# Index and attention scores of two heads as 64-row products on the two halves of the TensorE array

## The chip, the cores and the metric

The kernel runs on one core of a Trainium2 chip: TensorE (PE, with its weight loads shown apart as PEld), VectorE (DVE), ScalarE (ACT), GpSimd (POOL) and SyncE (SP), which issues the DMAs. The metric is the device time of one execution in microseconds. Three runs of the kernel before gave 1805.31, 1814.39 and 1805.31 us, so the median is 1805.31 us.

## The reference, cut to what matters

One layer of a hybrid decoder is computed for 1024 prompt tokens and 8 sampled tokens. Two of its parts are touched by the change, and both are products of queries and keys over a head dimension of 64:

```python
def select_keys(iq, ik, iw, qpos, topk):              # 8 index heads of 64, one key head
    dots = jnp.einsum('bqhd,bsd->bqhs', iq, ik)
    score = jnp.einsum('bqhs,bqh->bqs', jax.nn.relu(dots * IDX_DIM ** -0.5), iw) * IDX_HEADS ** -0.5
    ...                                                # causal mask, then the 256 best keys of each query
def sparse_attend(q, ksel, vsel, valid):              # 8 heads of 64 in two groups, one key head each
    logits = jnp.einsum('bqngd,bqknd->bqngk', qg, ksel) * HEAD_DIM_A ** -0.5
    ...                                                # mask, softmax, product with the values
```

The projections, the gated delta branch, the merge, the feed-forward part and the caches' work are as they were.

## The kernel before, in words

All in float32. A float32 operand is held in two parts, hi (rounded to the one-pass type fp32r) and lo (what is left), and a product is the sum of products of parts. `split` makes the two parts: ACT writes hi, DVE subtracts for lo.

Scores are made in two stages. **The index stage** (about 52 to 185 us of the span): for each of the query tiles i = 2 to 7 (128 queries), `scores` makes, per index head, the products with the 128·(i+1) keys so far, in one chunk up to 512 keys and in two halves above. ACT takes the relu, DVE sums over the heads with the weights. Beside it run the projections of later tiles and of z as filler (`mm3`, lines 163 to 165, tile `pj`), which keep TensorE fed. **The attention stage** (about 650 to 880 us): for each query tile i = 7 down to 0 and each of two groups of four heads, `att_scores` makes the logits of a head the same way (chunks into tile `PT`), DVE adds the mask and takes the row minimum, ACT takes the exponential, and then one of the two scales by the sum. `ORDER` is the order of these steps for four heads (0 = score, 1 = exp, 2 = norm). `att_out` transposes the weights (L1055, `PT` too) and multiplies by the values (L1059, L1060); it is woven with the scores of the next group, and the gates' projections and the sampled tokens' state update are filler.

How a score is made: `stack_q` puts hi of a head's 64 query rows on partitions 0 to 63 and lo on 64 to 127 for even heads, the other way round for odd heads. The keys stand doubled, the same 64 rows on both halves, hi in one plane and lo in another (`ik2`, `k2`). So two products of 128 rows, one with each plane, sum all four products of parts (L410 and L411 in the index stage, L1023 and L1024 in attention).

```python
nc.tensor.matmul(p, lhs, self.ik2[:, 0, c0:c1], start=True, stop=False)
nc.tensor.matmul(p, lhs, self.ik2[:, 1, c0:c1], start=False, stop=True)
```

The code's order is not the order on the engines: a scheduler (`schedule_with_timeline_sim`) puts the instructions of each engine into a fixed order when the program is built, from its own idea of when operands and buffers come free. PSUM holds 3 buffers of tile `ac` for the index scores and 5 of `PT` for attention.

Of the kernel before, what the change touches and what calls it, by code (L numbers as in the profile page):

```python
# [9 lines left out]
F32 = mybir.dt.float32  # L10
F32R = mybir.dt.float32r
# [3 lines left out]
AF = mybir.ActivationFunctionType  # L15
ALU = mybir.AluOpType
# [4 lines left out]
T = 1032  # L21
# [22 lines left out]

NORM_ACT = (0, 3)
RECIP = {0: 2, 2: 2}
ORDER = [(0, 0), (0, 1), (1, 0), (1, 1), (0, 3), (2, 0), (0, 2), (2, 1), (1, 2), (1, 3), (2, 2), (2, 3)]


BESIDE, PVS = 21, 8  # L50
# [4 lines left out]
class K:  # L55
# [205 lines left out]
    def stack_q(self, dst, nat, n, p):  # L261


        nc = self.nc
        m = nat.shape[1] // 2
        for j in range(m):
            nc.tensor.transpose(p[:, j, :n], nat[:, 2 * j:2 * j + 2, :].rearrange("p a b -> p (a b)"), self.ident[:n, :n])
        for e, (a, b) in enumerate(((0, 64), (64, 0))):
            nc.scalar.activation(dst[a:a + 64, e::2, :], p[a:a + 64, :m, :n], AF.Copy)
            nc.vector.tensor_tensor(dst[b:b + 64, e::2, :], p[a:a + 64, :m, :n], dst[a:a + 64, e::2, :].bitcast(F32),  # L270
                                    op=ALU.subtract)


    def p0_p1(self):
# [99 lines left out]
    def idx_proj(self, i, wA, wB):  # L374
        nc, wk, O = self.nc, self.wk, self.O
        r0, n = rows_of(i)
        nat = wk.tile([128, 592], F32, name="nat", tag="nat", bufs=2)
        for (wh, wl), c0 in ((wA, 0), (wB, 296)):
            if i < 2 and c0 == 0:
                continue  # L380
            p = self.pproj()
            self.mm3(p[:n, :296], [(self.xhi[:, k, r0:r0 + n], self.xlo[:, k, r0:r0 + n], wh[:, k], wl[:, k])
                                   for k in range(8)])
            nc.scalar.activation(nat[:n, c0:c0 + 296], p[:n, :296], AF.Copy)
        nc.vector.tensor_copy(self.ab[:n, i, :], nat[:n, 576:592])
        h0 = 8 if i < 2 else 0
        X = nat[:n, h0 * 64:576].rearrange("p (h d) -> p h d", d=64)
        self.rope(X, n, i, 1, 9 - h0)
        if i == 8:
            nc.sync.dma_start(O['ik_s'][0, :, 0, :], nat[:n, 512:576])  # L390
            nc.vector.tensor_copy(self.iqs, nat[:8, 0:576])
            return
        nc.sync.dma_start(O['ik_p'][0, 0, r0:r0 + n, :], nat[:n, 512:576])
        p = self.ptq()
        self.dup_T(nat[:n, None, 512:576], n, 1, p)
        self.split(self.ik2[:, 0, r0:r0 + n], self.ik2[:, 1, r0:r0 + n], p[:, 0, :])
        if i >= 2:
            self.iq2 = wk.tile([128, 8, 128], F32R, name="iq2", tag="iq2", bufs=2)
            self.stack_q(self.iq2, nat[:n, 0:512].rearrange("p (h d) -> p h d", d=64), n, self.ptq())

    def scores(self, i):
        nc, wk = self.nc, self.wk
        nk = 128 * (i + 1)
        ch = [(0, nk)] if nk <= 512 else [(0, nk // 2), (nk // 2, nk)]
        for c0, c1 in ch:
            Sv = self.S[:, self.soff[i] + c0:self.soff[i] + c1]
            for h in range(8):
                p = self.pacc()[:, :c1 - c0]
                lhs = self.iq2[:, h, :]
                nc.tensor.matmul(p, lhs, self.ik2[:, 0, c0:c1], start=True, stop=False)  # L410
                nc.tensor.matmul(p, lhs, self.ik2[:, 1, c0:c1], start=False, stop=True)  # L411
                r = self.relu[:, 512 * self.relu_n:512 * self.relu_n + c1 - c0]
                self.relu_n = 1 - self.relu_n
                nc.scalar.activation(r, p, AF.Relu, scale=0.125 * 8 ** -0.5)
                w = self.ab[:, i, h:h + 1]
                if h == 0:
                    nc.vector.tensor_scalar(Sv, r, w, 0.0, op0=ALU.mult, op1=ALU.add)
                else:
                    nc.vector.scalar_tensor_tensor(Sv, r, w, Sv, op0=ALU.mult, op1=ALU.add)
        d = self.S[:, self.soff[i] + 128 * i:self.soff[i] + nk]  # L420
        nc.gpsimd.affine_select(d, d, pattern=[[-1, 128]], compare_op=ALU.is_ge, fill=NEG, base=0,
                                channel_multiplier=1)
# [481 lines left out]
    def attention(self, end_x):  # L904
        nc, I = self.nc, self.I
        ps, end_ps = self.pool("fillers", space=PSUM)
        self.pq = self.pf = ps
        self.pj_bufs = 1
        self.ps, end_pa = self.pool("att", space=PSUM)
        self.ap, end_a = self.pool("att")  # L910
        self.sd, end_sd = self.pool("sampled")
        last, last_n = iter(()), 0
        for i in ATT:
            for g in range(2):
                P = [None] * 4
                weave(self.att_scores(i, g, P), 13, last, last_n)
                last, last_n = self.att_out(i, g, P), i + 2
        weave(last, last_n)
        gates = list(self.gates)
        weave(self.gate_steps(gates), 5 * len(gates), self.sample_delta(), 13)  # L920
        end_x()
        end_sd()
        mg, end_mg = self.pool("mergeg")
        self.wk, self.end_sa = self.pool("sample", side="right")
        mp, end_m = self.pool("mergeb", side="right")
        steps = self.merge_b(self.load_split(mp, self.d_ob), mg)
        self.sample = self.sample_attend(mg)
        weave(islice(self.sample, 33), 25, islice(steps, BESIDE), BESIDE)
        end_pa()
        end_ps()  # L930
        self.pj_bufs, self.tp_bufs = 5, 2
        self.open_psum("ps5")
        self.pf, self.end_pf = self.pool("psm", space=PSUM)
        self.stage = self.sp.tile([128, 2048], F32, name="rs", tag="kvb", bufs=1)
        x0 = self.sp.tile([128, 4224], F32, name="x20", tag="S", bufs=1)
        self.x2h = [x0[:, 0:4 * T].rearrange("p (j t) -> p j t", j=4)]
        self.x_T(0)
        self.pq = self.ps
        for _ in steps:
            pass  # L940
        end_m()
        end_mg()
        end_a()
# [61 lines left out]
    def att_scores(self, i, g, P):  # L1005

        nc, ap = self.nc, self.ap
        t0, nk = 128 * i, 128 * (i + 1)
        if g == 0:
            self.qn = ap.tile([128, 512], F32, name="qn", tag="qn", bufs=1)  # L1010
            nc.sync.dma_start(self.qn, self.d_q[t0:t0 + 128])
        q2 = ap.tile([128, 4, 128], F32R, name="q2", tag="q2", bufs=2)
        self.stack_q(q2, self.qn[:, 256 * g:256 * g + 256].rearrange("p (h d) -> p h d", d=64), 128, self.pT())
        ch = [(0, nk)] if nk <= 512 else [(0, nk // 2), (nk // 2, nk)]
        m0 = self.moff[i]
        st = ap.tile([128, 2, 2, 4], F32, name="st", tag="st", bufs=3)
        ng, sm = st[:, 0], st[:, 1, 0]

        def score(j):
            P[j] = ap.tile([128, T], F32, name="P", tag="P", bufs=8)  # L1020
            for c, (a, b) in enumerate(ch):
                p = self.pL()[:, :b - a]
                nc.tensor.matmul(p, q2[:, j, :], self.k2[:, g, 0, a:b], start=True, stop=False)  # L1023
                nc.tensor.matmul(p, q2[:, j, :], self.k2[:, g, 1, a:b], start=False, stop=True)  # L1024
                nc.vector.tensor_tensor_reduce(P[j][:, a:b], p, self.msk[:, m0 + a:m0 + b], -0.125,
                                               3e38 if c == 0 else ng[:, 0, j:j + 1], ALU.add, ALU.min,
                                               ng[:, c, j:j + 1])

        def exp(j):
            nc.scalar.activation(P[j][:, :nk], P[j][:, :nk], AF.Exp, scale=-1.0, bias=ng[:, len(ch) - 1, j:j + 1],  # L1030
                                 accum_out=sm[:, j:j + 1])

        def norm(j):
            if j in RECIP:
                v = sm[:, j:j + RECIP[j]]
                nc.vector.reciprocal(v, v)
            if j in NORM_ACT:
                nc.scalar.activation(P[j][:, :nk], P[j][:, :nk], AF.Copy, scale=sm[:, j:j + 1])
            else:
                nc.vector.tensor_scalar(P[j][:, :nk], P[j][:, :nk], sm[:, j:j + 1], None, op0=ALU.mult)  # L1040
        for f, j in ORDER:
            (score, exp, norm)[f](j)
            yield
# [788 lines left out]
```

## Time and profile before

| what | value |
|---|---|
| median of three runs | 1805.31 us |
| the profiled execution: its own time | 1802.74 us |
| its span, first to last instruction | 1801.0 us |
| PE busy (share of the span) | 1740.0 us (97%) |
| DVE, ACT busy | 1210.6 us, 852.1 us |
| mean granted TensorE clock | 0.995 |
| score products: index, attention | 160, 192 |

The span is shorter than the execution's time by 1.7 us, which lie around it. PE's "busy" is the union of its matmuls' modelled durations; consecutive matmuls overlap in it (a row's duration is about twice the distance to the next row's start), so the distance between starts, and not the duration, is what one matmul costs in a stream. In a row of a timeline the first number is the start in us, the second the duration, then come engine, line, operation, the tile written and those read, and the shape: `32*128` is the number of array rows and columns in use, `128x344` the operand that streams. A float32 product that isn't fp32r shows as two matmuls.

### The profile page before, as it was taken

The numbers are of one execution on the slowest core, as the hardware profiler recorded it, in microseconds if no ns is written. First come the engines' busy times: TensorE is split into PE (matmuls) and PEld (weight loads), VectorE is DVE, ScalarE is ACT, GpSimd is POOL, SyncE is SP. The second block draws the span as 40 slices with busy tenths as digits, with TensorE's granted clock in tenths as the row PEclk, the third lists the DMA queues.
The fourth block names the chain that finished last, engine by engine and source line by source line (L and its number), as shares of the span: only waits on it lengthen the run. The fifth ranks groups of instructions, "written<-read, shape, count | busy, mean of one in ns | idle before, by whom it ended". The sixth has DMA issues, their size and how long they took to land.

```text
span 1801.0 us, 31724 instructions
## 1 busy us (share of the span) xinstructions
PE 1740.0 (97%) x12276; PEld 1662.6 (92%) x12276; DVE 1210.6 (67%) x2776; ACT 852.1 (47%) x1575; POOL 42.2 (2%) x68
## 2 busy tenths in 40 slices
PE   5998999999999999999999999999999999999998
PEld 5998989999999988878899998999999999999998
DVE  7775558999899777797656477766666665733222
ACT  4567467877845345687444243433333333412012
POOL 3001100000000000000000000000000000000000
PEclk9999999999999999999999999999999999999999
DMA  6115434434546543254567434322222323732122
GB/s 194 43 35 153 130 101 145 130 113 120 159 131 167 149 137 109 84 183 141 195 235 226 138 110 135 101 81 85 82 72 75 91 72 125 223 100 73 51 80 69
DMA packets 293595, 218.01 MB, mean 121 GB/s; under 512 B 39292, under 2 KB 267456, under 8 KB 292412
## 3 DMA queue, kind: packets, MB, share of 16 engines
q1 hardware_dynamic: 291716, 205.50, 37.8%
q0 software_dynamic: 1728, 10.49, 1.7%
q8 instruction: 96, 1.57, 0.4%
q14 instruction: 55, 0.45, 0.1%
HBM read 154.17 MB, written 61.87 MB: 120 GB/s over the span
## 4 chain that ended last, share of the span: by engine, by line
PE 83%; DMA 7%; DVE 5%; ACT 3%; issue 2%; SPq 0%; ACTq 0%; DVEq 0%
PE pj L163 15%; PE pj L165 15%; PE pj L164 15%; PE A L1706 2%; PE A L1707 2%; PE A L1708 2%; PE D L1706 2%; PE F L1706 2%; PE F L1707 2%; PE D L1707 2%; PE F L1708 2%; PE D L1708 2%; PE PT L1055 1%; DMA araw<-d_act 1%; PE B L1706 1%
## 5 line engine op out<-in xcount | busy, mean ns | idle before, releaser
L163 PE MATMUL pj<-xhi,whi 128*128 128x344 f32 x912 | 297.5, 326 | 5.3 <-ACT gs L862 4.3
L165 PE MATMUL pj<-xhi,wlo 128*128 128x344 f32 x912 | 294.3, 323 | 0.0
L164 PE MATMUL pj<-xlo,whi 128*128 128x344 f32 x912 | 293.3, 322 | 0.0
L187 ACT ACTIVATE whi<-wraw 128x1024 fp32r<-128x1024 f32 (+4 forms) x126 | 115.2, 914 | 249.4 <-PE pj L164 208.0
L163 PEld LDWEIGHTS pj<-xhi,whi 128*128 128x128 f32 x912 | 171.9, 189 | 9.3 <-ACT gs L862 5.7
L164 PEld LDWEIGHTS pj<-xlo,whi 128*128 128x128 f32 x912 | 171.9, 188 | 2.0 <-issue 1.1
L165 PEld LDWEIGHTS pj<-xhi,wlo 128*128 128x128 f32 x912 | 171.9, 188 | 1.4
L164 PE MATMUL pj<-act,whi 128*128 128x344 f32 x528 | 170.3, 323 | 0.7 <-DVE act L188 0.7
L165 PE MATMUL pj<-act,wlo 128*128 128x344 f32 x528 | 168.9, 320 | 0.8 <-DVE wlo L188 0.8
L163 PE MATMUL pj<-act,whi 128*128 128x344 f32 x528 | 169.3, 322 | 0.2 <-DVE x L1768 0.2
L188 DVE TENSOR_TENSOR wlo<-wraw,whi 128x1024 fp32r<-128x1024 f32 (+3 forms) x104 | 116.2, 1118 | 54.4 <-ACT whi L187 52.7
L1768 DVE TENSOR_TENSOR x<-pj,x 128x344 f32<-128x344 f32 x96 | 48.5, 514 | 140.0 <-PE pj L165 139.9
L768 DVE TENSOR_SCALAR_CACHE_REDUCE kvb<-S,cand 128x384 bf16<-128x384 f32 (+3 forms) x128 | 103.7, 810 | 2.0
L165 PEld LDWEIGHTS pj<-act,wlo 128*128 128x128 f32 x528 | 99.2, 188 | 1.5 <-DVE wlo L188 1.3
L164 PEld LDWEIGHTS pj<-act,whi 128*128 128x128 f32 x528 | 99.2, 188 | 1.0 <-DVE act L188 1.0
L163 PEld LDWEIGHTS pj<-act,whi 128*128 128x128 f32 x528 | 99.2, 188 | 0.9 <-issue 0.4
L1706 PE MATMUL D<-hb,wx 128*128 128x258 f32 x328 | 93.0, 284 | 2.0 <-DVE E L1729 2.0
L1708 PE MATMUL D<-hb,wx 128*128 128x258 f32 x328 | 92.7, 282 | 0.7 <-DVE wx L188 0.7
L1706 PE MATMUL A<-hb,wlo 128*128 128x258 f32 x328 | 93.0, 283 | 0.0
L1707 PE MATMUL A<-hb,wlo 128*128 128x258 f32 x328 | 92.8, 283 | 0.0
L1708 PE MATMUL A<-hb,wlo 128*128 128x258 f32 x328 | 92.8, 283 | 0.0
L1707 PE MATMUL D<-hb,wx 128*128 128x258 f32 x328 | 92.6, 282 | 0.0
(587 smaller groups left out, 4790.3 us busy)
## 6 DMA issues: line engine op xcount, KB each, us to landing
wraw<-in_w_gate_up SPq DMA_DIRECT2D x50, 512.0 KB
wraw<-in_w_in SPq DMA_DIRECT2D x38, 512.0 KB
d_act<-x SPq DMA_DIRECT2D x41, 258.0 KB
araw<-d_act SPq DMA_DIRECT2D x20, 516.0 KB
d_g<-gs SPq DMA_DIRECT2D x48, 172.0 KB
wraw<-in_w_out SPq DMA_DIRECT2D x16, 512.0 KB
wraw<-in_w_branch SPq DMA_DIRECT2D x12, 512.0 KB
wraw<-in_w_down SPq DMA_DIRECT2D x16, 384.0 KB
```

The costliest lines, as they stand in the source:

```text
L163: nc.tensor.matmul(ps, lh, rh, start=(j == 0), stop=False)
L164: nc.tensor.matmul(ps, lh, rl, start=False, stop=False)
L165: nc.tensor.matmul(ps, ll, rh, start=False, stop=(j == last))
L187: self.nc.scalar.activation(hi, src, AF.Copy)
L188: self.nc.vector.tensor_tensor(lo, src, hi.bitcast(F32), op=ALU.subtract)
L768: nc.vector.tensor_scalar(junk[:r, :n], s, thr[:r, j:j + 1], 0.0, op0=ALU.is_lt, op1=ALU.add, accum_out=cnt[:r, j:j + 1])
L1055: nc.tensor.transpose(p[:, j, :], P[j][:, 128 * s:128 * s + 128], self.ident)
L1706: nc.tensor.matmul(p, lh, rh, start=(first and k == 0), stop=False, skip_group_check=True)
L1707: nc.tensor.matmul(p, lh, rl, start=False, stop=False, skip_group_check=True)
L1708: nc.tensor.matmul(p, ll, rh, start=False, stop=(k == 3), skip_group_check=True)
L1768: nc.vector.tensor_tensor(xv, p, xv, op=ALU.add)
```

## The change

Instead of two products of 128 rows per head and chunk there are three of 64 rows: hi·hi, hi·lo and lo·hi (the product of the two lo parts is left out). Two heads of a pair stand on the two halves: the even head on array rows 0 to 63, the odd one on 64 to 127. `pair_scores` writes them in turn, a product of the one head and then of the other, into two PSUM buffers. `stack_q` becomes a transpose and one `split`, with each head on its own half and the two parts in two planes. `score(j)` makes heads j and j+1, so that `ORDER` has ten steps instead of twelve, and the weave counts 11 instead of 13.

```diff
-ORDER = [(0, 0), (0, 1), (1, 0), (1, 1), (0, 3), (2, 0), (0, 2), (2, 1), (1, 2), (1, 3), (2, 2), (2, 3)]
+ORDER = [(0, 0), (1, 0), (1, 1), (0, 2), (2, 0), (2, 1), (1, 2), (1, 3), (2, 2), (2, 3)]
...
-        for e, (a, b) in enumerate(((0, 64), (64, 0))):
-            nc.scalar.activation(dst[a:a + 64, e::2, :], p[a:a + 64, :m, :n], AF.Copy)
-            nc.vector.tensor_tensor(dst[b:b + 64, e::2, :], p[a:a + 64, :m, :n], dst[a:a + 64, e::2, :].bitcast(F32),
-                                    op=ALU.subtract)
+        self.split(dst[:, 0, :, :n], dst[:, 1, :, :n], p[:, :m, :n])
+
+    def pair_scores(self, ps, q, j, k):
+
+        x = ((0, 0), (0, 1), (1, 0))
+        for i, (e, f) in enumerate(x):
+            for h, p in enumerate(ps):
+                r = slice(64 * h, 64 * h + 64)
+                self.nc.tensor.matmul(p, q[r, e, j], k[r, f], start=(i == 0), stop=(i == 2))
...
-            for h in range(8):
-                p = self.pacc()[:, :c1 - c0]
-                lhs = self.iq2[:, h, :]
-                nc.tensor.matmul(p, lhs, self.ik2[:, 0, c0:c1], start=True, stop=False)
-                nc.tensor.matmul(p, lhs, self.ik2[:, 1, c0:c1], start=False, stop=True)
...
+            for j in range(4):
+                ps = [self.pacc()[:, :c1 - c0] for _ in range(2)]
+                self.pair_scores(ps, self.iq2, j, self.ik2[:, :, c0:c1])
+                for h, p in zip((2 * j, 2 * j + 1), ps):
...
             for c, (a, b) in enumerate(ch):
-                p = self.pL()[:, :b - a]
-                nc.tensor.matmul(p, q2[:, j, :], self.k2[:, g, 0, a:b], start=True, stop=False)
-                nc.tensor.matmul(p, q2[:, j, :], self.k2[:, g, 1, a:b], start=False, stop=True)
...
+                ps = [self.pL()[:, :b - a] for _ in range(2)]
+                self.pair_scores(ps, q2, j // 2, self.k2[:, g, :, a:b])
```

The scheduler orders the new products anew. On TensorE in the index stage, at the tile of 320-key chunks, there stood (`ac` is the score's PSUM tile, `ik` and `iq` the keys and queries, `pj` a projection):

```order
L410 MATMUL ac<-ik_118,iq_837 128x320
L411 MATMUL ac<-ik_118,iq_837 128x320
L164 MATMUL pj<-xlo,whi 128x344
L165 MATMUL pj<-xhi,wlo 128x344
L370 MATMUL tp<-ident,x 128x8 x6
L410 MATMUL ac<-ik_118,iq_837 128x320
L411 MATMUL ac<-ik_118,iq_837 128x320
L410 MATMUL ac<-ik_118,iq_837 128x320
L411 MATMUL ac<-ik_118,iq_837 128x320
```

and at the same tile there stands now (L276 is the product in `pair_scores`):

```order
L276 MATMUL ac<-ik_118,iq_849 128x320 x3
L163 MATMUL pj<-xhi,whi 128x344
L164 MATMUL pj<-xlo,whi 128x344
L276 MATMUL ac<-ik_118,iq_849 128x320 x3
L267 MATMUL tq<-ident,nat 128x128
L276 MATMUL ac<-ik_118,iq_849 128x320 x3
L267 MATMUL tq<-ident,nat 128x128 x3
L165 MATMUL pj<-xhi,wlo 128x344
```

The six products of a pair, written in turn, stand as three of the one head and three of the other, with 128-row work between them. On TensorE in attention, at the tile of 448-key chunks (`PT` scores and transposes, `PV` the product with the values, `ph` and `pl` its operand's parts), there stood:

```order
L1060 MATMUL PV<-pl,v_6586 128x512
L1023 MATMUL PT<-k_6585,q_7163 128x448
L1024 MATMUL PT<-k_6585,q_7163 128x448
L1023 MATMUL PT<-k_6585,q_7163 128x448
L1024 MATMUL PT<-k_6585,q_7163 128x448
L1055 MATMUL PT<-ident,P 128x128 x4
```

and now:

```order
L1064 MATMUL PV<-ph,v_6654 128x512
L276 MATMUL PT<-k_6653,q_7243 128x448 x7
L1065 MATMUL PV<-pl,v_6654 128x512
L276 MATMUL PT<-k_6653,q_7243 128x448 x3
L1064 MATMUL PV<-ph,v_6654 128x512
L163 MATMUL pj<-xhi,whi 128x344
L164 MATMUL pj<-xlo,whi 128x344
```

Here runs of seven and of three products stand between the products with the values. Outside these two stages the order of every engine is as it was.

## Rows read from the trace of the kernel before

**Rows 1.** The page, busy time by engine, and the chain's engines.

```profile
PE 1740.0 (97%) x12276; PEld 1662.6 (92%) x12276; DVE 1210.6 (67%) x2776; ACT 852.1 (47%) x1575; POOL 42.2 (2%) x68
...
PE 83%; DMA 7%; DVE 5%; ACT 3%; issue 2%; SPq 0%; ACTq 0%; DVEq 0%
```

**Rows 2.** Busy time by stretch: from:to, length, each engine's, clock, DMA.

```profile
52.00:185.00 133.00, 127.88 (x815) 119.43 (x814) 91.57 (x209) 88.77 (x161) 8.80 (x15) 0.99 0.26 73
...
650.00:880.00 230.00, 227.29 (x1356) 191.44 (x1356) 185.48 (x501) 155.82 (x326) 7.55 (x8) 1.00 0.42 133
```

**Rows 3.** Instructions of lines 410 and 1023, with their shapes and counts.

```profile
L410 PE MATMUL ac<-ik,iq x80: 304/363/575, 56.3 to 181.3; 128*128 128x384 f32 x24, 128*128 128x512 f32 x24, 128*128 128x320 f32 x16, 128*128 128x448 f32 x16
...
L1023 PE MATMUL PT<-k,q x96: 222/366/500, 654.3 to 874.6; 128*128 128x512 f32 x24, 128*128 128x384 f32 x24, 128*128 128x448 f32 x16, 128*128 128x320 f32 x16
```

**Rows 4.** Timeline of PE, consecutive score products of 512 and of 384 keys.

```profile
655.35 0.39 PE L1023 MATMUL PT<-k,q 128*128 128x512 f32 x1
655.58 0.39 PE L1024 MATMUL PT<-k,q 128*128 128x512 f32 x1
...
736.63 0.34 PE L1023 MATMUL PT<-k,q 128*128 128x384 f32 x1
736.80 0.34 PE L1024 MATMUL PT<-k,q 128*128 128x384 f32 x1
```

**Rows 5.** Timeline of PE around a product on 32 array rows.

```profile
691.17 0.32 PE L165 MATMUL pj<-xhi,wlo 128*128 128x344 f32 x1
691.42 1.12 PE L1495 MATMUL tq<-sum,skv 32*128 32x512 f32 x2
692.47 0.47 PE L1023 MATMUL PT<-k,q 128*128 128x448 f32 x1
692.78 0.36 PE L1024 MATMUL PT<-k,q 128*128 128x448 f32 x1
```

**Rows 6.** Timeline of PE, float32 products of 512 columns on all rows.

```profile
224.73 1.88 PE L1281 MATMUL tx<-st,c 128*128 128x512 f32 x4
226.45 0.60 PE L1277 MATMUL tp<-ident,us 128*128 128x128 f32 x4
```

**Rows 7.** Timeline of PE around products on 64 rows and columns.

```profile
469.00 0.32 PE L164 MATMUL pj<-xlo,whi 128*128 128x344 f32 x1
469.25 0.68 PE L1117 MATMUL pi<-T,Btl 64*64 64x64 f32 x8
469.86 0.42 PE L165 MATMUL pj<-xhi,wlo 128*128 128x344 f32 x1
470.12 0.32 PE L163 MATMUL pj<-xhi,whi 128*128 128x344 f32 x1
```

**Rows 8.** Timeline of PEld in the same place.

```profile
469.25 0.54 PEld L1117 LDWEIGHTS pi<-T,Btl 64*64 64x64 f32 x8 [0.21 <-ACT kvb L765]
469.86 0.19 PEld L165 LDWEIGHTS pj<-xhi,wlo 128*128 128x128 f32 x1
469.96 0.19 PEld L163 LDWEIGHTS pj<-xhi,whi 128*128 128x128 f32 x1
470.12 0.19 PEld L164 LDWEIGHTS pj<-xlo,whi 128*128 128x128 f32 x1
```

**Rows 9.** Timeline of PE around float32 transposes on all rows.

```profile
672.66 0.32 PE L163 MATMUL pj<-xhi,whi 128*128 128x344 f32 x1
672.82 0.60 PE L1055 MATMUL PT<-ident,P 128*128 128x128 f32 x4
673.17 0.41 PE L164 MATMUL pj<-xlo,whi 128*128 128x344 f32 x1
673.42 0.32 PE L165 MATMUL pj<-xhi,wlo 128*128 128x344 f32 x1
```

**Rows 10.** ACT's part of stack_q: instructions of line 269.

```profile
L269 ACT ACTIVATE q<-PT x32: 363/379/382, 650.2 to 872.1; 64x256 fp32r<-64x256 f32 x32
L269 ACT ACTIVATE iq<-tq x12: 591/593/597, 52.3 to 129.8; 64x512 fp32r<-64x512 f32 x12
```

## What is predicted

> **What bounds the kernel now.** I read the page first: its line of busy times and the engines of the chain that ended last [rows 1]. PE is busy for 97% of the span, DVE for 67%, ACT for 47%, and 83% of the chain is PE. Then the table by stretch for the two stages in which scores are made, because an average over the span says nothing of them [rows 2]: PE is busy for 127.9 of 133 us in the index stage and for 227.3 of 230 in attention, at a granted clock of 0.99 and 1.00, while DVE has 31 and 19% free. So in both stages only 5.1 and 2.7 us of PE idle stand, and what the change adds to PE's stream it adds to the time, up to these few us. ACT and DVE are waited for little; what they save is worth next to nothing.
>
> **What the score products cost now.** PE's cost is read from the distance of starts. Two products of 512 keys stand 0.23 us apart, of 384 keys 0.17 [rows 4]; in between I put 0.20 for 448 and by the same line 0.14 for 320. The index stage has 80 products on each of its two lines, 24 of 384, 24 of 512, 16 of 320, 16 of 448 [rows 3]: 2 × (24 × 0.17 + 24 × 0.23 + 16 × 0.14 + 16 × 0.20) = 30.1 us. Attention has the same 80 and 16 more of 128 and 256 keys on each line, at about 0.11, the distance at which weight loads follow each other [rows 8]: 30.1 + 2 × 16 × 0.11 = 33.6 us. Together 63.7.
>
> **Part 1: three products for two.** A 64-row product streams as many columns as one of 128 rows, so one after another three cost half more: +15.0 us in the index stage, +16.8 in attention, +31.8. They are to come back by running the two heads beside each other: at best three slots for four. But that takes products of both halves next to each other, and the new order on PE mostly does not have that: a pair's six stand there as three of one head and three of the other with projections between. I went through the built program's list of PE instructions, in which each carries its half. The 528 products stand in 135 unbroken runs, 70 in the index stage and 65 in attention. Only 11 and 38 of these hold both halves at all, and inside them the half changes 24 and 119 times. So most of the extra slots cannot be hidden, whatever the array does.
>
> What can be hidden is bounded from both sides. If a product waits for the one before it whatever its half, nothing: +31.8. If it may start as soon as its own half is free and its weights are there, I walk each run with the distances above. With loads one after another at 0.11 (469.86 to 469.96 [rows 8]), 3.2 us come back in the index stage and 9.4 in attention: +19.2. An example: a run that changes half at every product, at 512 keys, needs 6 × 0.23 = 1.38 us in sequence, and 5 × 0.11 + 0.23 = 0.78 side by side. With the loads side by side as well, 3.4 and 13.5 come back: +14.9. No row of this trace has two halves next to each other, so the nearest row is that of the loads, and I take the middle value, +19.2.
>
> The Trainium skill says in TensorEngine Tiling (Array Packing), Key Properties, that tiles operate independently and can load weights and multiply in parallel. By that rule the sum would be the lower end, 4 us less than mine; no row here shows it either way.
>
> **Part 2: changing the shape of the array.** Around each run PE goes from 128-row work to 64-row work and back, and the trace shows what that costs. Before a product on 32 rows, the last projection takes from 691.17 to 691.42, 0.25 us where 0.16 is its distance [rows 5, 9]. The two passes of that product take until 692.47, 1.05 us where two such passes take 2 × 1.72/4 = 0.86 [rows 5, 6]. The first score after it takes 0.31 where 0.20 is usual [rows 5]. The excess is 0.09 + 0.19 + 0.11 = 0.39 us for the way in and out. Around products on 64 rows the same ends are there: 469.00 to 469.25 is 0.09 too long, 469.86 to 470.12 is 0.10 too long [rows 7], and the load behind the run begins only with its matmul and not one matmul ahead as in a stream (469.86 on both engines; the next one's load starts at 469.96, 0.16 ahead of its matmul at 470.12) [rows 7, 8]. So PE drains, and then the first weight load lies bare, once each way. It isn't the type that does it: float32 transposes on all rows between two fp32r projections fit without a gap, 672.66 to 673.42 is 0.76 for 2 × 0.16 + 4 × 0.11 [rows 9].
>
> The built list has 184 changes of the array's shape before and 424 after, 240 more. At 0.39/2 each that is +46.8 us. The lower bound is zero (if a 64-row product of full width changes nothing); with the drains alone, 0.09 each, it is 22. An upper one: if a change of half inside a run drains as well, 143 × 0.09 = 13 more. I take 46.8, since both shapes the trace has show the same excess.
>
> **Part 3: the rest.** `stack_q` has half as many instructions on twice the partitions: ACT loses 6 × 0.59 + 16 × 0.38 = 9.6 us [rows 10], DVE about as much. Both lie beside PE; a little of PE's idle may go with it. PSUM: a pair needs two of three index buffers at once, so PE may wait for ACT's relu; but PE will be slower and ACT is not, so I cost it at nothing, and with the cover gone at some 80 × 0.1 us. Nothing moves on SP's or POOL's queue of DMAs outside of the two stages. Of PE's 7.8 us of idle in the two stages about half should be filled by the longer work: −4.
>
> **The sum.** 46.8 + 19.2 − 4 = +62 us, on the profiled execution's 1802.74 (span 1801.0 and 1.7 around it): 1864.7. The median of the runs shown is 2.6 above that execution, so 1867.
>
> **The rivals.**
>
> *The halves never overlap.* Then part 1 costs its full 31.8: 46.8 + 31.8 − 4 = +75, 1880, and 1893 if a change of half drains too. For it: in the streams of [rows 4, 9] each product waits for the one before. Against it: those share their rows of the array, and no row has two halves next to each other.
>
> *The change of shape is cheaper for 64 rows by 128 columns.* Rows 5 and 7 are float32 products, and none has this shape with fp32r. With drains alone the sum is 22 + 19 − 4 = +37, 1842; with no cost at all 14.9 to 19.2 less 4, about 1820. Against it: both shapes show the drain, and the type is ruled out by rows 9.
>
> *Not slower: PE's queue takes the second head's run ahead.* If the three products of the second half were started beside the first head's, past the projections that stand between, every pair would need three slots for four: −63.7/4 = −16 us, 1789. It decides only if it holds in nearly all runs: the shape changes must vanish too, and from 240 changes at more than 0.07 us each the gain is gone. Against it: in all timelines the starts are in the order of the program, and a projection of 128 rows leaves no half free.
>
> *The change doesn't do what it says* is in part my forecast: the text writes pairs in turn, the built order keeps them so in 49 of 135 runs.
>
> **How the numbers follow.** My forecast 0.47; no overlap 0.30; cheaper changes of shape 0.18; not slower 0.05. The likeliest gives 1867, itself within some 10 us by the two load cases and the idle. The no-overlap case reaches 1880 to 1893, the cheap case 1820 to 1842; a range of 1826 to 1893 leaves out part of the cheap case, the not-slower case and little above. Half a per cent, 9 us, is about what a measurement of this kernel can tell from no change. All cases but the last are slower by more than that: slower 0.95, the same 0.02, faster 0.03.
>
> **What the new profile would show.** Right: PE still busy for nearly all of both stages, the index stage longer by some 35 us and attention by some 28, everything after shifted alone. Around a run of L276 the projection ahead stands some 0.09 us too long and the first one behind some 0.10; a run of three at 320 keys takes about 0.8 us with its ends. In a run with both halves two starts stand nearer together than 0.14 us. Wrong in part 1 if starts there are never nearer than the columns; wrong in part 2 if the projections around a run keep 0.16; wrong altogether if PE shows new idle instead, waiting for PSUM or for DVE, or if the granted clock falls below 0.99 in a stage, which would add time that no term here has.

## The result and the profile after

The changed kernel takes 1880.47 us, median of four runs (1877.71 to 1883.59), the kernel before in the same comparison 1808.28 us (1805.31 to 1814.39). The ratio is 1.0397, with a 95% interval of 1.0365 to 1.043: slower, by about 72 us. The forecast was 1867 us in a range of 1826 to 1893. The profiled execution took 1879.01 us with a span of 1877.3 us, 76.3 us more span than before.

The page of the changed kernel, its busy times, the granted clock in 40 slices and the engines of the chain, beside [rows 1]:

```profile
PE 1808.7 (96%) x12452; PEld 1677.5 (89%) x12452; DVE 1199.1 (64%) x2754; ACT 839.1 (45%) x1549; POOL 43.5 (2%) x68
...
PEclk9999899999999989999989999999999999999999
...
PE 83%; DMA 8%; DVE 5%; ACT 2%; issue 1%; SPq 1%; POOL 0%; DVEq 0%; ACTq 0%; POOLq 0%
```

PE is still the bound: its busy time grew by 68.7 us, its idle time from 61.0 to 68.6. ACT's busy time fell by 13.0 us, where 9.6 was forecast, and that changes nothing. New are slices in which the clock stands at 8 tenths.

The table by stretch of the changed kernel, in the columns of [rows 2]: the index stage, attention, the stretch from the last product with the values to the softmax of the sampled keys, and two short stretches inside:

```profile
52.00:219.00 167.00, 162.13 (x890) 125.37 (x889) 90.38 (x209) 83.06 (x154) 9.65 (x15) 0.97 0.21 58
685.00:934.00 249.00, 247.78 (x1396) 187.97 (x1395) 175.22 (x482) 148.91 (x307) 6.87 (x7) 0.97 0.38 118
936.10:969.90 33.80, 25.68 (x137) 20.87 (x136) 12.12 (x24) 7.17 (x12) 1.89 (x2) 0.91 0.56 195
196.10:206.30 10.20, 8.74 (x27) 6.77 (x26) 4.43 (x6) 7.89 (x11) 0.00 (x0) 0.50 0.34 112
694.40:708.10 13.70, 13.70 (x57) 10.84 (x58) 7.78 (x27) 6.92 (x11) 0.00 (x0) 0.50 0.46 134
```

PE has 4.9 us of idle in the index stage where it had 5.1, so the longer work filled hardly any of it. All 4.9 are two waits of a score product for a PSUM buffer, which ACT's relu frees; the longer of them stands here:

```profile
195.44 1.15 PE L276 MATMUL ac<-ik,iq 64*128 64x512 f32 x3 [3.41 <-ACT gr L418]
```

The granted clock fell from 0.99 and 1.00 to 0.97 in both stages, because of stretches at 0.50, the 1.2 GHz level. The one at the end of the index stage (196.1) begins just behind that idle; the one at the start of attention (694.4) has PE busy throughout. The third row is the other surprise. Before, that stretch was this:

```profile
882.30:892.10 9.80, 9.80 (x63) 9.53 (x61) 5.83 (x14) 2.02 (x4) 0.82 (x1) 1.00 0.88 289
```

It is 24 us longer now: 74 more PE instructions stand in it (15.9 us of busy time) and 8.1 us in which PE has nothing to do. The products of the sampled keys used to be done before the last product with the values and now end after it. Their softmax comes next, and of the projections that cover such gaps 18 matmuls are left in the built order between the last of these products and the transposes of the softmax, where 60 stood. So the order of PE behind attention is not as it was, against what is said under "The change": work that used to stand among the scores stands behind them. The list of waits of the changed kernel in that stretch:

```profile
PE pj L164 <- DVE oa L188: 5.0, 1, 5.0
PE tq L1377 <- DVE sPn L1370: 1.4, 1, 1.4
PE pj L163 <- ACT oa L187: 1.4, 1, 1.4
```

Read by landmarks (first and last start of a stage's instructions in either trace), the changed kernel is late by 34.4 us at the end of the index stage, 35.3 at the first attention score, 50.4 at the last one, 53.8 at the last product with the values, 77.8 at the softmax of the sampled keys, and 76.3 at the end. (The end of the index stage is the first start of the transposes that follow it, 197.7 us before and 232.1 now.)

The counts of line 276, which answer to [rows 3]: 240 and 288 products where 160 and 192 stood.

```profile
L276 PE MATMUL PT<-k,q x288: 269/366/792, 689.6 to 925.2; 64*128 64x512 f32 x36, 64*128 64x384 f32 x36, 64*128 64x448 f32 x24, 64*128 64x320 f32 x24
...
L276 PE MATMUL ac<-ik,iq x240: 299/386/793, 55.4 to 206.6; 64*128 64x384 f32 x36, 64*128 64x512 f32 x36, 64*128 64x320 f32 x24, 64*128 64x448 f32 x24
```

The timeline of PE in the changed kernel, a run of three of one head in the index stage, and a run of six in attention in which the halves alternate:

```profile
102.82 0.30 PE L163 MATMUL pj<-wA,xhi 128*128 128x296 f32 x1
103.05 0.70 PE L276 MATMUL ac<-ik,iq 64*128 64x320 f32 x3
103.67 0.41 PE L164 MATMUL pj<-wA,xhi 128*128 128x296 f32 x1
103.92 0.30 PE L165 MATMUL pj<-wA,xlo 128*128 128x296 f32 x1
...
760.83 0.88 PE L276 MATMUL PT<-k,q 64*128 64x448 f32 x6
761.64 0.42 PE L163 MATMUL pj<-xhi,whi 128*128 128x344 f32 x1
```

The first run: the projection ahead stands 0.23 us from it where 0.135 is the distance of such projections, the run takes 0.62 where three times 0.14 is 0.42, and the projection behind takes 0.25. The excess is 0.095 + 0.20 + 0.115 = 0.41 us, where 0.39 was forecast from [rows 5, 7]. The second run: six products of 448 keys in 0.81 us, which is three slots of 0.20 and a drain of 0.2. So the halves overlap, completely. Such a pair's two starts lie mostly 2 to 4 ns apart in the records, those of their weight loads too, and the next pair's 0.23 us later at 512 keys.

The weight loads of the first run, in the changed kernel's timeline of PEld, answer to [rows 8]:

```profile
103.04 0.44 PEld L276 LDWEIGHTS ac<-ik,iq 64*128 64x128 f32 x3 [0.17 <-issue]
103.67 0.19 PEld L164 LDWEIGHTS pj<-wA,xhi 128*128 128x128 f32 x1 [0.19 <-issue]
103.78 0.19 PEld L165 LDWEIGHTS pj<-wA,xlo 128*128 128x128 f32 x1
```

The first load on either side starts with its matmul and not ahead of it, as forecast.

### The profile page after: what moved, and what is told of

The parts are those of the page before. It is cut to its first block, busy times and chain, and to the rows that moved or that the text cites. A ratio compares the mean times of both kernels' runs of the same rounds, so it can differ in the third digit from the quotient of the medians.

```text
span 1877.3 us, 32045 instructions
## 1 busy us (share of the span) xinstructions
PE 1808.7 (96%) x12452; PEld 1677.5 (89%) x12452; DVE 1199.1 (64%) x2754; ACT 839.1 (45%) x1549; POOL 43.5 (2%) x68
## 4 chain that ended last, share of the span: by engine, by line
PE 83%; DMA 8%; DVE 5%; ACT 2%; issue 1%; SPq 1%; POOL 0%; DVEq 0%; ACTq 0%; POOLq 0%
PE pj L163 15%; PE pj L165 14%; PE pj L164 14%; PE PT L276 3%; PE ac L276 2%; PE F L1711 2%; PE D L1711 2%; PE F L1712 2%; PE D L1712 2%; PE F L1713 2%; PE D L1713 2%; PE A L1711 2%; PE A L1712 2%; PE A L1713 2%; PE PT L1060 2%; DMA gt<-d_g 2%
```

## The experiments

**Theory A**, after the result: a change of the array's shape costs 0.195 us, the halves overlap, and the columns that are not beside each other cost in sequence; what lies beyond is half clock and lost cover. **Theory B**: the halves don't overlap (the rival that gave 1880). **Theory C**: the change of shape is not what costs, but the products themselves, their order and their waits. **Theory D**: the lost cover behind attention costs some 10 us or more by itself. Later: E, the lost cover comes from the index stage; F, the half clock comes with the drains; G, the cost lies in each 64-row product and not in the changes. In each, the interval is that of the ratio, and the spans are of the profiled executions.

### samehalf: both heads on one half

```diff
-                r = slice(64 * h, 64 * h + 64)
+                r = slice(0, 64)
```

> Both heads of a pair are put on array rows 0 to 63, so that no two products can overlap; the order on every engine is that of the changed kernel, with the same 424 changes of the array's shape. (The odd head's scores are computed from the even head's rows.) Theory A, the halves overlap in full in the changed kernel: the 16.9 us that overlap gave back are lost, 1880 + 17 = 1897. Theory B, overlap gave back nothing and the changed kernel's 75 us are shape changes plus all extra columns: no difference, 1880 (within 4).

Measured: 1916.51 us against 1806.33, ratio 1.0579 (1.0531 to 1.0627). Its order on PE is that of the changed kernel. A run of six as above, in its timeline of PE:

```profile
761.25 1.48 PE L276 MATMUL PT<-k,q 64*128 64x448 f32 x6
762.66 1.12 PE L1500 MATMUL tq<-sum,skv 32*128 32x512 f32 x2
```

1.41 us where the changed kernel has 0.81: six slots and the drain. So the overlap is real and B falls, although B's time, 1880, was the one measured. The loss of 36 us was larger than A's 17; the table by stretch of this kernel shows where more may come from, a long stretch at half clock at the start of attention:

```profile
696.60:730.70 34.10, 34.10 (x110) 27.59 (x110) 15.07 (x53) 10.13 (x15) 0.00 (x0) 0.50 0.30 87
```

### full128: three products on all rows

```diff
-                r = slice(64 * h, 64 * h + 64)
+                r = slice(0, 128)
```

> Three products per head as in the changed kernel, but each over all 128 rows, so that the shape of the array does not change at scores (186 changes in all, 184 before the change) and nothing can overlap. (Each score then sums the two heads of the pair.) Theory A and B alike, a change of shape costs 0.195 us: 1808 + 31.8 of columns - 4 = 1836, that is 47 less than with both heads on one half once the lost cover of some 10 us is also put aside: 57 less than samehalf. Theory C, the loss is not the change of shape but the order, the PSUM waits and the clock: within 20 us of samehalf, so above 1870.

Measured: 1840.03 us against 1806.33, ratio 1.0179 (1.0135 to 1.0223), 4 us from the expectation; the index stage ended 15.3 us late, where 15.0 was the price of its third products. Up to 685 us the order on PE is that of the changed kernel, so on PE the two index stages differ in the rows of their scores alone: 19.1 us between them, where 120 changes at 0.195, less the 3.4 of overlap, make 20.0. Its timeline of PE has no excess around a run of three:

```profile
102.30 0.31 PE L163 MATMUL pj<-wB,xhi 128*128 128x296 f32 x1
102.45 0.60 PE L276 MATMUL ac<-ik,iq 128*128 128x320 f32 x3
102.89 0.30 PE L164 MATMUL pj<-wB,xhi 128*128 128x296 f32 x1
```

0.44 us for the three, 0.62 above. C falls: three products for two explain 34 us even in sequence, and the changed kernel lost 72.

### two: the third product left out

```diff
-        x = ((0, 0), (0, 1), (1, 0))
+        x = ((0, 0), (0, 1))
...
-                self.nc.tensor.matmul(p, q[r, e, j], k[r, f], start=(i == 0), stop=(i == 2))
+                self.nc.tensor.matmul(p, q[r, e, j], k[r, f], start=(i == 0), stop=(i == 1))
```

> The changed kernel with the third product (lo by hi) left out: as many columns per head as before the change, 352 products in 139 runs, 439 changes of the array's shape, 255 more than before the change. Theory A: 255 x 0.195 = 50 us for the shape, less 8.6 that full overlap gives back, plus some 6 us of lost cover behind the sampled keys: 1808 + 47 = 1855. Theory C, what costs is the number of products and not the shape: near 1808.

Measured: 1867.52 us against 1806.33, ratio 1.0325 (1.0283 to 1.0368). With as many products as before, on half the rows, the kernel is still 61 us slower, so C falls here too. A was 12 us too low; half clock stood for 67.4 us of this span and for 19.5 before.

### middle: only the second of three products on 64 rows

```diff
-                r = slice(64 * h, 64 * h + 64)
+                r = slice(64 * h, 64 * h + 64) if i == 1 else slice(0, 128)
```

> As full128 (three products on all 128 rows, which sums other parts than the reference asks for), but the middle one of the three on 64 rows: 489 changes of the array's shape in the program against 186 in full128 and 424 with 64 rows throughout, with a third of the 64-row time of samehalf. Theory A (a change of shape costs 0.195 us whatever the run is, and the half clock comes with 64-row work): full128's 32 us, 303 x 0.195 = 59 more, and a third of the 30 us that samehalf lost beyond its changes: +101, about 1910 us beside a kernel before of 1808. Rival F (the half clock comes with the drains): 32 + 59 + 30 x 303/238 = +129, about 1937 us, with more half-clock time than samehalf's 89 us. Rival G (not the change of shape costs but each 64-row product, a load or a partial row group being slow): a third of the 76 us between samehalf and full128 on top of full128, +57, about 1865 us.

Measured: 1909.94 us against 1807.38, ratio 1.057 (1.0529 to 1.0611), where A said 1910. The timeline of PE in this kernel:

```profile
108.35 0.30 PE L163 MATMUL pj<-wA,xhi 128*128 128x296 f32 x1
108.48 0.99 PE L276 MATMUL ac<-ik,iq 128*128 128x320 f32 x3
109.31 0.30 PE L164 MATMUL pj<-wA,xhi 128*128 128x296 f32 x1
```

Here the changes lie inside the run (the row names the shape of its first product): no gap ahead of it and none behind, but 0.83 us for three products that need 0.42, so two changes cost 0.41. One product on 64 rows costs as much excess as three or six in a row, so G falls. Half clock stood for 66.6 us, less than samehalf's 100.3 with more changes, and in all four runs the mean granted clock was higher here (0.982 and 0.983) than there (0.974 to 0.979): F falls too.

### idxonly and attonly: one stage at a time

The edit gives one stage back the two products of 128 rows and the old `stack_q` (and `ORDER`, for attention), as in the diff of the change read backwards. For idxonly in attention:

```diff
-                ps = [self.pL()[:, :b - a] for _ in range(2)]
-                self.pair_scores(ps, q2, j // 2, self.k2[:, g, :, a:b])
+                p = self.pL()[:, :b - a]
+                nc.tensor.matmul(p, q2[:, j, :], self.k2[:, g, 0, a:b], start=True, stop=False)
+                nc.tensor.matmul(p, q2[:, j, :], self.k2[:, g, 1, a:b], start=False, stop=True)
```

> Only the index scores are made as 64-row products of pairs; attention is as in the kernel before. Theory A (the costs are those of the two stages, one beside the other): the index stage of the changed kernel ended 34 us late, so about 1808 + 34 = 1842 us; the stretch between the last product with the values and the softmax of the sampled keys keeps the 9.8 us of the kernel before, since its cover of projections is not used up. Rival E (the second stage is late because the first one is: the work that it uses as filler was spent there): the tail is longer here as well, 1842 + some 20 = 1862 us. Half the TensorE clock: theory A has one or two stretches in or behind the index stage, none at the start of attention.

> Only the attention scores are made as 64-row products of pairs; the index stage is as in the kernel before. Theory A: the changed kernel lost 41 us between the first attention score and the softmax of the sampled keys, 15 to the last score, 3.5 to the last product with the values, 24 behind it, so about 1808 + 41 = 1849 us, with the half-clock stretch at the start of attention (10 to 25 us) and the softmax again more than 25 us behind the last product with the values. Rival E (the lost cover comes from the index stage): only the first 18 us, 1826 us.

Measured, both against 1812.95: idxonly 1845.78 us, ratio 1.0196 (1.0168 to 1.0223); attonly 1854.13 us, ratio 1.0244 (1.0216 to 1.0272). The spans are 35.1 and 42.6 us longer than before, together 77.7, where the changed kernel has 76.3: the two stages' costs add up. The stretch from the last product with the values to the softmax, first in idxonly, then in attonly, with attonly's start of attention:

```profile
921.30:931.10 9.80, 9.80 (x63) 9.51 (x61) 5.85 (x14) 2.02 (x4) 0.84 (x1) 1.00 0.89 288
```

```profile
898.80:933.30 34.50, 29.64 (x159) 23.24 (x157) 13.51 (x26) 7.88 (x13) 2.83 (x3) 0.98 0.65 217
658.70:672.40 13.70, 13.70 (x59) 11.15 (x59) 8.00 (x27) 6.75 (x12) 0.00 (x0) 0.50 0.47 134
```

The late softmax belongs to attention's change alone: E falls. The stretch at half clock at the start of attention stands here as well, with the index stage as it was.

### hold: the cover kept for the softmax

The merge's projections, which cover the softmax of the sampled keys, are tied behind the last product of the sampled keys, and the weave beside them takes 40 steps in place of 25.

```diff
+            m = nc.tensor.matmul(ps, lh, rh, start=(j == 0), stop=False)
+            if self.hold is not None and j == 0 and last == 3:
+                self.tc.add_manual_dep(m.ins, self.hold, mybir.DependencyInfo(
...
-        weave(islice(self.sample, 33), 25, islice(steps, BESIDE), BESIDE)
+        weave(islice(self.sample, 33), 40, islice(steps, BESIDE), BESIDE)
...
+                    if q == 3 and half == 1:
+                        self.hold = m.ins.name
```

> The changed kernel, but the last steps of the merge's first product are kept behind the last product of the sampled keys, so that 58 of its matmuls stand between that and the softmax transposes, as 60 do in the kernel before and 18 in the changed one. Theory D, about 10 us of the loss is that the scheduler used this filler up earlier, so that PE stands bare during the sampled softmax and the clock falls there: 1880 - 10 = 1870, range 1866 to 1874. If the gap is set by something else (a transfer of the merge, or the drained pools): no change, 1880.

Measured: 1882.6 us against 1806.33, ratio 1.0395 (1.0348 to 1.0441): no change from the changed kernel's. The table by stretch of this kernel, to the softmax and from there to the gate and up projections:

```profile
936.00:957.40 21.40, 17.57 (x89) 12.34 (x87) 8.07 (x16) 5.00 (x9) 1.89 (x2) 1.00 0.56 192
957.40:1194.50 237.10, 221.54 (x1673) 213.08 (x1673) 140.14 (x247) 84.60 (x135) 0.94 (x1) 0.96 0.50 159
```

The first stretch is 12.4 us shorter than in the changed kernel (it is taken from the same time on; the last product with the values itself starts at 938.7 here). The second is 19.4 longer than its 217.7: the work that was held stands there (70 more instructions), and PE idles 15.6 us in it, 10.9 before. So the long stretch at the softmax was in large part work in another place, and D falls as a cost of its own.

### inturn: the pair's products kept in turn

```diff
+        last = None
+        dep = mybir.DependencyInfo(mybir.DependencyClass.NoSync, mybir.DependencyReason.DATA)
...
-                self.nc.tensor.matmul(p, q[r, e, j], k[r, f], start=(i == 0), stop=(i == 2))
+                m = self.nc.tensor.matmul(p, q[r, e, j], k[r, f], start=(i == 0), stop=(i == 2))
+                if last is not None:
+                    self.tc.add_manual_dep(m.ins, last.ins.name, dep, reason="in turn")
+                last = m
```

> As the changed kernel, but the six products of a pair are kept in turn (one head, the other, one head ...), so that 357 changes of the array's shape stand in the program where the changed kernel has 424, in 101 runs that nearly all change half at each product. Theory A (shape 0.195 us a change, halves overlap with their loads): 67 x 0.195 = 13 us less for the shape, and the columns of the two stages fall from 81 to about 52 us by the distances of the trace: 1880 - 13 - 28 = about 1840 us; if the new order has more waits for the PSUM buffers, up to 1860. Rival B (no real overlap): 1880 - 13 = 1867 us. In both the first start of the second head in a pair stands less than 0.02 us behind the first head's if they overlap, one product later if not.

Measured: 1859.78 us against 1812.95, ratio 1.0283 (1.0247 to 1.032). That is 47 us slower than before, where the changed kernel was 72, so 25 of the 40 us that A expected came. In the timeline of PE each pair now costs what one head cost in the changed kernel, six products in 0.64 us where three took 0.62:

```profile
99.55 0.30 PE L164 MATMUL pj<-wB,xhi 128*128 128x296 f32 x1
99.77 0.70 PE L278 MATMUL ac<-ik,iq 64*128 64x320 f32 x6
100.41 0.40 PE L165 MATMUL pj<-wB,xlo 128*128 128x296 f32 x1
100.65 0.30 PE L163 MATMUL pj<-wB,xhi 128*128 128x296 f32 x1
```

By landmarks the index stage ends 20.2 us earlier than in the changed kernel, and the way from the first attention score to the softmax is 18.5 us shorter: together 38.7, near the 41 that A said. But the parts are not A's. A's own terms give some 34 of it in the index stage, which has 80 changes less, and some 5 in attention; and the 18.5 come out of the softmax's stretch, which is back to 10.1 us from 33.8. What the index stage lacks stands at its end, where 77 products follow each other with no projection between. They begin at 175.27 and the last ones at 193.81, where three slots a pair make 8.5 us in all. PE's rows there, ACT's relu, and the waits of the weight loads between 170 and 200 us:

```profile
175.27 0.87 PE L278 MATMUL ac<-ik,iq 64*128 64x448 f32 x6
176.58 0.91 PE L278 MATMUL ac<-ik,iq 64*128 64x448 f32 x6 [0.43 <-ACT gr L423]
...
193.81 0.97 PE L278 MATMUL ac<-ik,iq 64*128 64x512 f32 x5 [0.36 <-ACT gr L423]
```

```profile
180.28 0.54 ACT L423 ACTIVATE gr<-ac 128x448 f32<-128x448 f32 x1 [0.24 <-DVE S L428]
181.06 0.55 ACT L423 ACTIVATE gr<-ac 128x448 f32<-128x448 f32 x1 [0.24 <-DVE S L428]
```

```profile
PEld ac L278 <- ACT gr L423: 10.4, 22, 0.8
```

A pair needs two of the three index buffers, and a buffer comes free with the relu, about every 0.78 us, since ACT itself waits for DVE's sum over the heads. So some 11 us are lost there: the waits for PSUM buffers that the expectation named, with up to 1860 us. The part between the stages takes 9.2 us longer than before: PE has 21 more instructions in it (2976 for 2955) and 4.3 us more idle. So some filler that covered the index stage is done later. With each pair in one run the changes still cost more than the overlap gives: 0.64 and the two ends' 0.21 is 0.85 us, where four products of 128 rows take 0.56.

## Why the prediction was right, and where not

**The direction, the bound and part 2: right.** PE bounds both stages and nothing hides what its stream gains. The change of shape was the largest term, 46.8 us from 0.39 us per run. The changed kernel's runs show 0.41, full128 shows the price in the index stage with the order on PE unchanged, and middle, with 303 more changes than full128, came out where 0.195 us a change put it. The index stage was forecast 35 us longer and is 34.4. Attention was forecast some 28 longer, with everything behind it shifted alone: from its first score to its last product with the values it is 18.5, and 24.0 come behind that.

**Part 1: right in kind, the wrong end.** That many of the third products stay in sequence was right, but "most of the extra slots cannot be hidden" said too much: by the same walk with full overlap 16.9 of the 31.8 us come back. I took the loads as coming one after another (+19.2), and they overlap: 0.81 us for six products of 448 keys is three slots, with no load between. The lower end, +14.9, is the one that runs, and the rule that I gave beside it (the Trainium skill, TensorEngine Tiling (Array Packing), Key Properties: tiles operate independently, loads too) is borne out by that 0.81.

**"−4" for PE's idle: wrong.** In the index stage the idle stayed (5.1 and 4.9 us), and over the span it grew by 7.6 us; 8.1 us of new idle stand ahead of the softmax of the sampled keys. I looked for idle that longer work fills, and not for what the new order puts elsewhere: the sampled keys' products share PE with attention, and slipped behind its end. The length of the work alone doesn't do that. full128 has a longer stream too and keeps 60 projections ahead of the softmax and a stretch of 13.8 us there, while two, with as many products as before, has 20 and 29.7. Why the order came out so was not looked into. And hold, which keeps 58, has as much idle in other places: PE stands idle for 67.3 us of its span, 68.6 in the changed kernel.

**A term that was missing: the clock.** I named a fall below 0.99 as something that no term has, and it came: 58.4 us of the span at 1.2 GHz, 19.5 before (both summed over the trace's clock records). If PE would have worked through all of these stretches at the upper level, half of the difference was lost, 19.5 us at most. A nearer figure comes from runs of the kernel before on one chip: with a mean granted clock of 0.993 and 0.994 they took 1807.71 and 1807.48 us, with 0.985 and 0.986 they took 1813.42 to 1814.67, some 8 us for 0.01. On the two other chips the same reading of the kernel before gives more, 12 and 14 (on one of them 1803.58 to 1806.97 us at 0.992 to 0.994, 1817.79 at 0.985). The changed kernel's profiled execution has 0.985, that of before 0.995, so I estimate 8 to 14. From the other side, PE's busy time grew by 68.7 us, of which the changes and the columns are 61.7 at their prices; that leaves 7.0 for the clock. The same sum, with the upper bound, for every kernel, against its profiled span, all as differences from the kernel before:

| kernel | changes of shape × 0.195 | columns | half clock ÷ 2 | sum | measured |
|---|---|---|---|---|---|
| after | 240: 46.8 | +14.9 | (58.4 − 19.5)/2 = 19.5 | 81 | 76.3 |
| samehalf | 240: 46.8 | +31.8 | (100.3 − 19.5)/2 = 40.4 | 119 | 113.6 |
| full128 | 2: 0.4 | +31.8 | (37.6 − 19.5)/2 = 9.1 | 41 | 35.1 |
| middle | 305: 59.5 | +31.8 | (66.6 − 19.5)/2 = 23.6 | 115 | 104.9 |
| two | 255: 49.7 | −8.6 | (67.4 − 19.5)/2 = 24.0 | 65 | 63.2 |
| hold | 244: 47.6 | +14.9 | (76.3 − 19.5)/2 = 28.4 | 91 | 83.8 |
| idxonly | 120: 23.4 | +11.6 | (33.0 − 19.5)/2 = 6.8 | 42 | 35.1 |
| attonly | 129: 25.2 | +4.7 | (57.0 − 19.5)/2 = 18.8 | 49 | 42.6 |
| inturn | 173: 33.7 | −11.4 | (45.4 − 19.5)/2 = 13.0 | 35 | 48.6 |

The changes are counted in the built programs, the columns walked over their runs with full overlap (in sequence for samehalf, full128 and middle). Eight of nine sums lie 2 to 10 us above the measurement, as they may where the clock's column is an upper bound; PE's idle, which differs by −2 to +10 us, is not in them. Only inturn lies below, by 13 us: it has the 11 us of waits at the end of its index stage and the longer stretch between its two stages, for which the sum has no term.

So the forecast for the profiled execution was +62 where 76.3 came: 62, less 4.3 for the loads side by side, plus 11.6 for idle that grew by 7.6 instead of falling by 4, plus 8 to 14 for the clock, is 77 to 83. The clock's part of that is the least certain; 19.5 would make it 89.

**The rivals.** "No overlap" gave the number that was measured, 1880, and is wrong: samehalf shows what it looks like, 36 us slower than the changed kernel. Its agreement is chance: the 17 us that it has too much for the columns stand for idle and clock, which it lacks. "Cheaper changes of shape" and "the second head's run taken ahead" are refuted by the run of three above: the excess is full, and all starts are in the order of the program.

**What stays open.** What makes the granted clock fall at the start of attention was not isolated. The stretch there is longer with 64-row scores in attention (attonly 13.7 us, the changed kernel 13.7, inturn 10.2, middle 17.1, two 23.9, hold 27.3, samehalf 34.1) than without (none in the kernel before, 3.4 in idxonly, 6.8 in full128 with 3.4 more just ahead), while PE works on scores and on two-column products of the sampled tokens' state in turn. But its length is not fixed by the order: up to 913 us hold has the changed kernel's order on PE, and twice its stretch, as the table by stretch of hold shows:

```profile
687.40:714.70 27.30, 27.30 (x109) 22.26 (x109) 14.28 (x52) 9.00 (x14) 0.00 (x0) 0.50 0.37 109
```

Each length is that of one execution, so inturn's 10.2 and full128's 6.8 can't be told apart, nor can it be said how much of samehalf's 34.1 comes from its halves.

## What to carry to other kernels

Before two half-height products are put beside each other, look in the built order at how long the runs are: here a run pays about 0.4 us for going into the other shape and out, whether it holds one product or six, and two products of 512 keys side by side give back 0.23 us. Write such pairs so that the scheduler must keep them together, or it may spread them as here, and see that filler or PSUM buffers are left for them, since in inturn some of the gain went into waits for buffers. Count the third product for what it is, half as many columns more. And when PE's order is made anew, look in it at the other chains that share PE, since here one of them ended late.

## What the runs showed of the hardware

Two 64-row fp32r products on the two halves start mostly 2 to 4 ns apart, their weight loads too; a change from 128 to 64 rows and back costs 0.39 to 0.41 us, 0.20 a change, in the runs looked at. The longest stretches at half clock stand in the kernels with 64-row scores in attention, and no idle of PE stands ahead of that fall: in the changed kernel PE was busy for 10.35 of the 10.4 us before it, and for all 13.7 us of the stretch. At its start, in the changed kernel's timeline of PE, twelve products of 512 keys in turn took 2.86 us at the 1.2 GHz level, 0.48 a pair:

```profile
704.72 2.93 PE L276 MATMUL PT<-k,q 64*128 64x512 f32 x12
707.58 0.87 PE L1060 MATMUL PT<-ident,P 128*128 128x128 f32 x4
```

At 2.4 GHz, before the clock fell, eight of them stood in 1.13 us from the first start to the next line's, 0.28 a pair with the drain:

```profile
689.63 1.20 PE L276 MATMUL PT<-k,q 64*128 64x512 f32 x8
690.76 0.61 PE L1470 MATMUL tq<-skq,S 128*128 128x2 f32 x4
```
